# Hybrid attention block: the rotated key's halves from the latent turns, ten dummy products at the start, and rotary query stores from ScalarE

## The chip, the cores and the metric

The kernel runs on one core of a Trainium2 chip. A core has five engines, each with its own queue of instructions that it works off strictly in order: TensorE (PE in the profile, its weight loads PEld), VectorE (DVE), ScalarE (ACT), GpSimd (POOL) and SyncE (SP), which here does nothing but issue DMAs. The metric is the time of one execution in microseconds (us) on the device; lower is better.

## What is computed

One block with two attention branches over 512 tokens with 16 learned meta tokens ahead of them (528 positions, 16 heads, model width 1024). Cut to what matters here:

```python
u = rmsnorm(h, pre_norm_g[l])
proj = u @ w_in[l]
(cq, ckv, k_pe_raw, z_mla, fq, fk, fv, f_logit, z_fox, gate_a, gate_b) = jnp.split(proj, split_idx, axis=-1)
q = (rmsnorm(cq, mla_q_norm_g[l]) @ w_uq[l])        # per head: 64 plain and 32 rotary columns
kv = (rmsnorm(ckv, mla_kv_norm_g[l]) @ w_ukv[l])
k_pe = rope(k_pe_raw, pos)[:, None]                 # one rotated key of 32 columns for all heads
q_m = jnp.concatenate([q_nope, rope(q_pe, pos)], axis=-1)
k_m = jnp.concatenate([k_nope, jnp.broadcast_to(k_pe, ...)], axis=-1)
o_mla = causal_block_attention(q_m, k_m, v_mla, MLA_SCALE)
log_f = jax.nn.log_sigmoid(f_logit + fox_forget_b[l])
cum = jnp.cumsum(log_f, axis=-1)                    # added to the fox scores
o_fox = causal_block_attention(fox_heads(fq), fox_heads(fk), fox_heads(fv), FOX_SCALE, cum)
y_mla = (o_mla * jax.nn.silu(z_mla)) @ w_br_mla[l]
y_fox = (o_fox * jax.nn.silu(z_fox)) @ w_br_fox[l]
mixed = (jax.nn.sigmoid(gate_a) * y_mla + jax.nn.sigmoid(gate_b) * y_fox) @ w_out[l]
h = h + rmsnorm(mixed, post_norm_g[l])
```

## The kernel before

**Halves.** A float32 product is made of three products in a shorter format: an operand is split into an upper half (a rounded copy, names ending in h, hi or wh) and a lower half (the remainder, l, lo or wl). Each weight tile of 128 x 1024 is loaded raw by SyncE (`wload`, L90 for its DMA), copied into wh by ScalarE (L127) and subtracted into wl by GpSimd (L128, recorded at the helper's line L102). Raw and split weight tiles have three buffers each. `mm` (L96) and `tps` (L99) are all products and transposes, so tiles are told apart by name.

**Order.** TensorE's order is written out by hand: both large stages stand under a manual schedule, and a PE instruction runs where the program has it. On the other engines the framework's scheduler decides at build time, by priority (program order, which `tc.high_priority(offset=...)` raises) and by its own estimate of when an operand is ready. `tc.issue_after(ins)` puts an instruction behind `ins` on the same engine, `tc.keep_in_program_order` pins one. The list `behind` holds an instruction behind which the wh casts (L126) are put.

**First stage (L261 to L519).** Five token tiles (0 to 3 of 128 tokens, 4 of the 16 meta tokens) are loaded, normed (`squares`, `scaled`), turned on PE (`turn`, tile pt), scaled by the gain and split into uTh and uTl (`turned`). `small` makes the 432 narrow columns of the projection (tile psm: query latent, key-value latent, rotary key, forget logits). `back` norms the latents and rotates the key on the token-major tile sm. `latent` turns sm into the PSUM tile pc, which has one buffer, and copies out: cTh by ScalarE (L433), cTl by VectorE (L434), the rotated key kpT (L435) and the forget logits fT (L436) by ScalarE. Then come the fox queries and keys of head pair 0 (`qk`, tiles fq and fk): 7 of their steps, the last latent, the forget chain, and the rest. `hl_done` splits such a product into hlq or hlk: ScalarE copies the upper half (L239), VectorE subtracts the lower one (L240, recorded at L102), and only then is the accumulator free. There are three accumulators of 512 columns (`acc`), used in turn by all projections.

The forget chain is Abs, Exp, Ln on ScalarE (L503 to L505), a combination (L506) and a running sum (L507) on VectorE, two halves ch (L510, L511), four DMAs into the tile CT (L516) and two into DRAM (L518). CT enters the fox scores through a product with ONE, a tile that holds ones in two rows of each half.

**Start of attention (L534 to L566).** The rotated key must stand in two tiles of 128 partitions, one 64-row half for each head of a pair: KPH holds the upper half of kpT four times (four VectorE copies, L560), KPL the lower half twice over zeroed rows (GpSimd L561, VectorE L563). Then `pe_unit(0)` makes the rotary queries of the first eight heads (tile ppe): products, VectorE multiplications by the rotary tables (L623), GpSimd sums and halves (`rest`, L628 to L631) into gT. Head pair 0's part goes to the tile QP by DMA; the other six heads' part is stored to DRAM (`store`, L641; L90 qpe_dram) and loaded again for each later pair.

**Attention stages.** Sixteen stages alternate fox and MLA for eight head pairs. Each makes scores (st) into sf, exponentials (L763), normed probabilities as two half-precision parts pn (L777 to L791), and transposes these by DMA into pt (`dma_start_transpose`, eight a stage, in SyncE's queue); values (`ov`) multiply pt by vp one stage later. Between them PE works off weight products of later stages (z, fq, mq, v, ...) from a list `fills`, in pieces. In stage 1 (first MLA stage) the four stores of the rotary queries are issued by SyncE, behind the second store of ch.

The last stages multiply by the branch and output weights; the change does not touch them.

Of the kernel before, what the change touches and what calls it, by code (L numbers as in the profile page):

```python
# [54 lines left out]
def block_kernel(ctx: ExitStack, tc: tile.TileContext, x, meta_tokens, pre_norm_g, w_in, fox_forget_b,  # L55
# [21 lines left out]
    padp.tile([128, 56], F32, tag="pad", name="pad")  # L77
# [23 lines left out]
    def split_lo(eng, lo, src, hi):  # L101
        eng.tensor_tensor(out=lo, in0=src, in1=f32(hi), op=ALU.subtract)  # L102
# [120 lines left out]
    nc.gpsimd.memset(f32(CT), 0.0)  # L223
# [37 lines left out]
    with ExitStack() as ph:  # L261
# [57 lines left out]
        kpT = pal.tile([ROPE, L], F32, tag="kpT", name="kpT")  # L319
# [5 lines left out]
        hns, sts, pts0 = {}, {}, {}  # L325
# [73 lines left out]
        def back(t):  # L399
# [6 lines left out]
            for a, b, i in both:  # L406

                nc.scalar.activation(sm[:rows, a:b], psm[:rows, a:b], AF.Square, scale=(b - a) ** -0.5,
                                     accum_out=st2[:rows, i : i + 1])
# [14 lines left out]
        def latent(t, sm):  # L424
            rows, d0, q0 = (128, META + 128 * t, 0) if t < 4 else (META, 0, R_Q)
            k0 = R_Q + R_KV
            pc = pps.tile([128, 4, 128], F32, tag="pc", name=f"pc{t}", bufs=1)
            i0 = q0 // 128
            for i in range(i0, 3):
                tps(pc[:, i, :rows], sm[:rows, 128 * i : 128 * i + 128], ident[:rows, :rows])  # L430
            tps(pc[0 : ROPE + NH, 3, :rows], sm[:rows, k0:NSM], ident[:rows, :rows])
            ds = slice(d0, d0 + rows)
            nc.scalar.copy(cTh[:, i0:3, ds], pc[:, i0:3, :rows])  # L433
            split_lo(nc.vector, cTl[:, i0:3, ds], pc[:, i0:3, :rows], cTh[:, i0:3, ds])  # L434
            nc.scalar.copy(kpT[:, ds], pc[0:ROPE, 3, :rows])  # L435
            nc.scalar.activation(fT[:, ds], pc[ROPE : ROPE + NH, 3, :rows], AF.Identity, bias=fb)  # L436
# [27 lines left out]
        for c in (2, 3):  # L464
# [33 lines left out]
        qk = q_fox(0) + k_fox(0)  # L498
        run(qk[:7])
# [19 lines left out]
        run(qk[7:])  # L519
# [14 lines left out]
    with ExitStack() as att:  # L534
# [8 lines left out]
        KP = [ac.tile([128, L], F32R, tag=n, name=n) for n in ("KPH", "KPL")]  # L543
# [15 lines left out]
        for r in range(4):  # L559
            nc.vector.tensor_copy(KP[0][32 * r : 32 * r + 32], kpT)  # L560
        nc.gpsimd.memset(f32(KP[1]), 0.0)  # L561
        for h in range(2):
            split_lo(nc.vector, KP[1][64 * h : 64 * h + 32], kpT, KP[0][0:32])  # L563
        lctx.close()
        gpool = gctx.enter_context(tc.tile_pool(name="gpool", bufs=1, side="right"))
        gT = [gpool.tile([128, KD, S], F32, tag=n, name=n) for n in ("gT0", "gT1")]  # L566
# [25 lines left out]
        def pe_unit(g):  # L592
            if g == 0:
                r0, tt = (p.rearrange("p a b -> p (a b)")[:, 0 : 8 * S].bitcast(F32).rearrange("p (c s) -> p c s", c=4)
                          for p in pts)
            else:
                r0, tt = gT[0][:, 4:8], gT[1][:, 4:8]
            rp = r0[:, 0:2]

            rr = [r0[:, 2:4], tt[:, 2:4]] if g else [t[:, 4:6] for t in gT]  # L600
            if g == 0:
                nc.sync.dma_start(rp, rope_pe)
# [8 lines left out]
            def srcs():  # L611
                if g:

                    tc.keep_in_program_order(nc.sync.dma_start(rp, rope_pe))
# [3 lines left out]
            for xi in range(2):  # L618
                get = (lambda: half(1)) if xi else weights(srcs, lambda ws: half(0, ws))

                def done(i, ps, xi=xi):
                    for cs in range(2):
                        nc.vector.tensor_tensor(out=tt[:, 2 * xi + cs], in0=ps, in1=rp[:, cs], op=ALU.mult)  # L623
                out += unit(f"ppe{g}{xi}", get, cq_act, 2, REAL, done)

            def rest(x):

                nc.gpsimd.tensor_tensor(out=tt[:, x], in0=tt[:, x], in1=tt[:, 3 - x], op=(ALU.subtract, ALU.add)[x])  # L628
                hi, lo = rr[x][:, 0], rr[x][:, 1]
# [4 lines left out]
                else:  # L634

                    for h in range(2):
                        for i in range(2):
                            r = 64 * h + 32 * i + 16 * x
                            dma(f32(QP[r : r + 16]), rr[x][16 * h : 16 * h + 16, i])
# [197 lines left out]
        pe, rest0, store0 = pe_unit(0)  # L837
        pe_rest = [(0, lambda x=x: rest0(x)) for x in range(2)]
        g = gate_unit()
        first = pe + v + [(0, in_order)] + g[:4]  # L840
# [23 lines left out]
        run(first)  # L864
        late = []
        for si, (br, pr) in enumerate(stages):
# [6 lines left out]
            if si == 0:  # L873
# [187 lines left out]
```

## Time and profile before

| | us |
|---|---|
| three runs | 621.47, 623.43, 623.82 |
| their median | 623.43 |
| the profiled execution | 622.67 |
| its span, first to last instruction | 620.9 |
| TensorE busy in it | 598.2 |
| ScalarE, VectorE, GpSimd busy | 330.6, 315.9, 265.2 |

A row of the timeline gives the start in us from the span's beginning, the duration in us, engine, line, operation, written tile, read tiles, shapes and how many instructions are merged in it; the bracket at its end is the time that the engine sat idle before it and what ended that. Matmuls overlap: each row lasts longer than the distance to the next. SPq is SyncE's queue, in which a DMA's row is its issue, not its transfer. The page's clock row gives the share of full speed that TensorE was granted.

### The profile page before, as it was taken

To read this page: it belongs to the slowest core of one execution; us is meant where nothing else is said; L and a number is where in the kernel's file an instruction comes from. 1 tells how busy PE (TensorE), PEld (TensorE's weight loads), DVE (VectorE), ACT (ScalarE), POOL (GpSimd) and SP (SyncE) were. 2 spreads that over 40 slices of the span, in tenths; PEclk is the share of its full clock that TensorE was granted. 3 is DMA by queue.
4 is the path that set the end of the run, shared out by engine and by line. 5 is a ranking of instruction groups with operands and counts; after the bars stand their busy time and mean duration, and the time that the engine had idled before them with its cause. 6 is when DMAs were issued, how large, how long until landed. Compare 5 with 4: busy or idle time off the path is not lost.

```text
span 620.9 us, 11001 instructions
## 1 busy us (share of the span) xinstructions
PE 598.2 (96%) x3811; PEld 508.3 (82%) x3811; DVE 315.9 (51%) x922; ACT 330.6 (53%) x757; POOL 265.2 (43%) x270
## 2 busy tenths in 40 slices
PE   4997999799999999999999999999999999999996
PEld 4886889688889889889888898887888888888885
DVE  3948657456666765764675657627321122024034
ACT  7855746556665765775676658646322222232321
POOL 4216636344345653444353523542644444444610
PEclk9999999799999999999999999999999999999998
DMA  8431579968987778879778696971433332333602
GB/s 277 93 95 51 116 174 145 219 158 169 172 180 143 168 182 169 192 172 184 151 165 182 145 174 155 189 170 34 136 102 101 102 95 86 92 103 120 253 34 102
DMA packets 223512, 89.31 MB, mean 144 GB/s; under 512 B 141708, under 2 KB 216852, under 8 KB 223456
## 3 DMA queue, kind: packets, MB, share of 16 engines
q1 hardware_dynamic: 223456, 88.61, 61.9%
q8 instruction: 30, 0.49, 0.3%
q14 instruction: 26, 0.21, 0.1%
HBM read 54.43 MB, written 4.00 MB: 94 GB/s over the span
## 4 chain that ended last, share of the span: by engine, by line
PE 85%; DVE 5%; ACT 3%; DMA 2%; issue 2%; SPq 1%; POOL 1%; DVEq 0%; ACTq 0%; POOLq 0%
PE pg L96 14%; PE py L96 14%; PE z L96 14%; PE v L96 8%; PE po L96 7%; PE fq L96 6%; PE fk L96 6%; PE st L96 5%; PE ov L96 3%; PE psm L96 3%; DVE sf L755 2%; PE mq L96 2%; SPq L90 1%; PE mk L96 1%; DMA ht<-in_x_dram 1%
## 5 line engine op out<-in xcount | busy, mean ns | idle before, releaser
L102 POOL TENSOR_TENSOR wl<-wraw,wh 128x1024 fp32r<-128x1024 f32 (+1 forms) x90 | 207.2, 2306 | 222.6 <-ACT wh L127 220.8
L127 ACT CAST wh<-wraw 128x1024 fp32r<-128x1024 f32 (+1 forms) x90 | 90.0, 1004 | 170.0 <-issue 48.1
L763 ACT ACTIVATE sf<-sf,nb 128x144 f32<-128x144 f32 (+3 forms) x128 | 72.0, 565 | 13.8 <-DVE nb L755 13.8
L791 DVE SCALAR_TENSOR_TENSOR pn<-sf,ri,pn 128x128 f16<-128x128 f32 (+3 forms) x128 | 68.7, 575 | 13.1 <-ACT pn L790 13.0
L790 ACT ACTIVATE pn<-sf,ri 128x128 f16<-128x128 f32 (+3 forms) x128 | 61.5, 551 | 19.9 <-ACT sf L763 17.9
L944 DVE SCALAR_TENSOR_TENSOR tb<-th,py 128x512 f32<-128x512 f32 x16 | 11.0, 687 | 101.9 <-PE py L96 101.9
L96 PE MATMUL st<-hlk,hlq 64*128 64x272 f32 (+3 forms) x480 | 51.0, 311 | 0.7 <-DVE nb L755 0.2
L96 PE MATMUL z<-uTh,wh 128*128 128x512 f32 x128 | 50.8, 397 | 0.0
L755 DVE CUSTOM_DVE_ANT_0 sf<-st,maskt 128x272 f32<-128x272 f32 (+2 forms) x128 | 48.4, 434 | 3.9 <-PE st L96 3.9
L96 PE MATMUL pg<-uTh,wh 128*128 128x512 f32 x128 | 50.2, 392 | 0.0
L96 PE MATMUL z<-uTh,wl 128*128 128x512 f32 x128 | 50.0, 391 | 0.0
L96 PE MATMUL z<-uTl,wh 128*128 128x512 f32 x128 | 49.9, 390 | 0.0
L96 PE MATMUL pg<-uTl,wh 128*128 128x512 f32 x128 | 49.8, 389 | 0.0
L96 PE MATMUL pg<-uTh,wl 128*128 128x512 f32 x128 | 49.8, 389 | 0.0
L96 PE MATMUL py<-gh,wh 128*128 128x512 f32 x128 | 49.8, 389 | 0.0
L96 PE MATMUL py<-gl,wh 128*128 128x512 f32 x128 | 49.8, 389 | 0.0
L96 PE MATMUL py<-gh,wl 128*128 128x512 f32 x128 | 49.8, 389 | 0.0
L777 POOL TENSOR_TENSOR mt<-sf,ri 128x96 f32<-128x96 f32 (+1 forms) x32 | 9.5, 296 | 85.9 <-DVE ri L772 72.3
L96 PEld LDWEIGHTS st<-hlk,hlq 64*128 64x128 f32 x480 | 37.2, 187 | 8.1 <-ACT wh L127 2.5
L96 PE MATMUL v<-uTh,wh 128*128 128x256 f32 (+1 forms) x128 | 36.6, 286 | 2.3 <-DVE hlk L102 2.3
L96 PE MATMUL ov<-pt,vp 128*64 128x512 f16 (+4 forms) x416 | 35.2, 318 | 3.5 <-DMA pt<-pn 3.5
L96 PEld LDWEIGHTS <-vp 128*64 128x64 f16 (+1 forms) x416 | 22.8, 113 | 17.5 <-issue 8.5
(189 smaller groups left out, 1419.5 us busy)
## 6 DMA issues: line engine op xcount, KB each, us to landing
wraw<-in_w_in_dram SPq DMA_DIRECT2D x56, 512.0 KB
wraw<-in_w_br_fox_dram SPq DMA_DIRECT2D x8, 512.0 KB
wraw<-in_w_br_mla_dram SPq DMA_DIRECT2D x8, 512.0 KB
wraw<-in_w_out_dram SPq DMA_DIRECT2D x8, 512.0 KB
pt<-pn SPq DMA_TRANSPOSE x128
xr<-in_x_dram SPq DMA_DIRECT2D x4, 512.0 KB
out_dram<-yo SPq DMA_DIRECT2D x8, 256.0 KB
QP<-qpe_dram SPq DMA_DIRECT2D x7, 256.0 KB
```

The lines of the kernel that those rows point to most:

```text
L90: ins = (start or nc.sync.dma_start)(out=out, in_=src)
L96: nc.tensor.matmul(*a, **k)
L102: eng.tensor_tensor(out=lo, in0=src, in1=f32(hi), op=ALU.subtract)
L127: nc.scalar.copy(wh[:, :n], raw[:, :n])
L755: nc.vector.tensor_tensor_reduce(out=sf_of(h, b)[:, c0 : c0 + w], in0=ps[h][:, o : o + w], in1=maskt[:, m0 : m0 + w], scale=-scale, scalar ...
L763: exps[g] = nc.scalar.activation(sf, sf, AF.Exp, bias=sums["nb"][:, h, b : b + 1], scale=-1.0, accum_out=sums["su"][:, h, b : b + 1]).ins
L777: nc.gpsimd.tensor_tensor(out=mt, in0=src, in1=ri.unsqueeze(3).broadcast_to([128, 2, nb_, META]), op=ALU.mult)
L790: nc.scalar.activation(hi, sf, AF.Copy, scale=rib)
L791: nc.vector.scalar_tensor_tensor(out=lo, in0=sf, scalar=rib, in1=hi, op0=ALU.mult, op1=ALU.subtract)
L944: nc.vector.scalar_tensor_tensor(out=tb[br], in0=ths[i, br], scalar=1.0, in1=py, op0=ALU.add, op1=ALU.mult)
```

## The change

It has five parts.

1. CT and ONE are cleared by VectorE instead of GpSimd, and ten products of ONE with 512 columns of CT are put first on PE, into an accumulator that nobody reads. The gain column's copy moves behind the scaling of the first token tile.
2. KPH and KPL are allocated early. `latent` writes their first 32 partitions straight from pc: the upper half by ScalarE in place of the copy kpT, the lower half by VectorE. All five operations of `latent` get a priority raised by 60, with ScalarE's three ahead of VectorE's two. KPL is zeroed at the start.
3. The four copies and two subtractions of L559 to L563 go. Four DMAs from SyncE spread the first 32 partitions: three for KPH, one for KPL. They stand behind the rotary query products in the program, as does the allocation of gT, so `pe_unit` now looks its tiles up when it runs.
4. From the seventh fox step on, the wh casts are put behind the square of tile 1's latents, until the rotary query products are through. The rest of `qk` moves ahead of ch, and ch behind the copy of the second half of hlk. An Exp of one element follows it.
5. The four stores of the rotary queries are issued by ScalarE, at the end of stage 0, two behind the copy hlq and two behind the second copy hlk of the first MLA pair.

```diff
+    KP = [fx.tile([128, L], F32R, tag=n, name=n) for n in ("KPH", "KPL")]
-    nc.gpsimd.memset(f32(CT), 0.0)
-    nc.gpsimd.memset(f32(ONE), 0.0)
+    nc.vector.memset(f32(CT), 0.0)
+    nc.vector.memset(f32(ONE), 0.0)
     for h in range(2):
-        nc.gpsimd.memset(f32(ONE[64 * h : 64 * h + 2, :]), 1.0)
+        nc.vector.memset(f32(ONE[64 * h : 64 * h + 2, :]), 1.0)
+    nc.gpsimd.memset(f32(KP[1]), 0.0)
...
-            nc.scalar.copy(cTh[:, i0:3, ds], pc[:, i0:3, :rows])
-            split_lo(nc.vector, cTl[:, i0:3, ds], pc[:, i0:3, :rows], cTh[:, i0:3, ds])
-            nc.scalar.copy(kpT[:, ds], pc[0:ROPE, 3, :rows])
-            nc.scalar.activation(fT[:, ds], pc[ROPE : ROPE + NH, 3, :rows], AF.Identity, bias=fb)
+            with tc.high_priority(offset=60):
+                nc.scalar.copy(cTh[:, i0:3, ds], pc[:, i0:3, :rows])
+                nc.scalar.copy(KP[0][0:ROPE, ds], pc[0:ROPE, 3, :rows])
+                nc.scalar.activation(fT[:, ds], pc[ROPE : ROPE + NH, 3, :rows], AF.Identity, bias=fb)
+                split_lo(nc.vector, cTl[:, i0:3, ds], pc[:, i0:3, :rows], cTh[:, i0:3, ds])
+                split_lo(nc.vector, KP[1][0:ROPE, ds], pc[0:ROPE, 3, :rows], KP[0][0:ROPE, ds])
...
+        spun = acc("spun")
+        for _ in range(10):
+            mm(spun, ONE, CT[:, 0:512], start=True, stop=True)
         gps = ppt.tile([128, 4, 128], F32, tag="pt", name="gps")
         tps(gps[:, 0, 0:KD], g8, ident[0:KD, 0:KD])
         squares(0, pin)
+        scaled(0, pin)
         pin(nc.vector.tensor_copy(gcol, gps[:, 0, 0:KD]))
-        scaled(0, pin)
...
         qk = q_fox(0) + k_fox(0)
+        behind[:] = [squared[1]]
         run(qk[:7])
         latent(3, sms[3])
...
+        run(qk[7:])
         ch = pal.tile([NH, 2, L], F32R, tag="ch", name="ch")
-        nc.scalar.activation(ch[:, 0], fa[:, 0], AF.Copy, scale=-1.0 / SC_FOX)
+        with tc.issue_after(halved[("k", 1, 0), 1]):
+            nc.scalar.activation(ch[:, 0], fa[:, 0], AF.Copy, scale=-1.0 / SC_FOX)
+            nc.scalar.activation(pad[0:1, 0:1], eps_t[0:1, 0:1], AF.Exp)
...
-        run(qk[7:])
...
-        for r in range(4):
-            nc.vector.tensor_copy(KP[0][32 * r : 32 * r + 32], kpT)
-        nc.gpsimd.memset(f32(KP[1]), 0.0)
-        for h in range(2):
-            split_lo(nc.vector, KP[1][64 * h : 64 * h + 32], kpT, KP[0][0:32])
...
-            def store(x, a, b):
+            def store(x, a, b, start=None):
                 for i in range(2):
-                    dma(qpe_dram[8 * g + a : 8 * g + b, i, x], rr[x][16 * a : 16 * b, i])
+                    dma(qpe_dram[8 * g + a : 8 * g + b, i, x], results(x)[16 * a : 16 * b, i], start)
...
-        run(first)
+        run(pe0)
+        behind.clear()
+        for r in (64, 32, 96):
+            nc.sync.dma_start(f32(KP[0][r : r + ROPE]), f32(KP[0][0:ROPE]))
+        nc.sync.dma_start(f32(KP[1][64 : 64 + ROPE]), f32(KP[1][0:ROPE]))
...
+        run(first[len(pe0) :])
...
                 run(fill[5:])
+                written[0] = False
+                for x in range(2):
+                    with tc.issue_after((halved[("q", 0, 0), 0], halved[("k", 0, 0), 1])[x]):
+                        store0(x, 2, 8, nc.scalar.dma_start)
+                written[0] = True
             else:
                 run(fill[:1])
-                if si == 1:
-
-                    written[0] = True
-                    for x in range(2):
-                        store0(x, 2, 8)
-                    written[0] = False
```

More of the change, by code (lines that the diff above doesn't have):

```diff
@@ L101, in split_lo @@
     def split_lo(eng, lo, src, hi):
-        eng.tensor_tensor(out=lo, in0=src, in1=f32(hi), op=ALU.subtract)
+        return eng.tensor_tensor(out=lo, in0=src, in1=f32(hi), op=ALU.subtract)
     def wload(srcs):
@@ L542, in block_kernel @@
         QP = ac.tile([128, S], F32R, tag="QP", name="QP")
-        KP = [ac.tile([128, L], F32R, tag=n, name=n) for n in ("KPH", "KPL")]
         maskt = ac.tile([128, L + 16], BF16, tag="maskt", name="maskt")
@@ L558, in block_kernel @@
             nc.gpsimd.memset(pn[b // 3][:, :, PN_STEP * b % 15, :], 0.0)
[L559 to L566 removed]
+        gT = []
         wuqh = wuq.rearrange("p k (h e) -> p k h e", e=NOPE + ROPE)
@@ L592, in pe_unit, with room, results @@
         def pe_unit(g):
-            if g == 0:
[L594 to L602, printed above, removed]
+            def room():
+                if g == 0:
+                    return [p.rearrange("p a b -> p (a b)")[:, 0 : 8 * S].bitcast(F32).rearrange("p (c s) -> p c s", c=4)
+                            for p in pts]
+                return gT[0][:, 4:8], gT[1][:, 4:8]
+            def results(x):
+                if g == 0:
+                    return gT[x][:, 4:6]
+                return room()[x][:, 2:4]
+            if g == 0:
+                nc.sync.dma_start(room()[0][:, 0:2], rope_pe)
             out = []
@@ L863, in block_kernel @@
         ahead(first + sum(fills, []) + tail)
-        run(first)
+        run(pe0)
[3 more added lines that the diff above has]
+        nc.sync.dma_start(f32(KP[1][64 : 64 + ROPE]), f32(KP[1][0:ROPE]))
+        lctx.close()
+        gpool = gctx.enter_context(tc.tile_pool(name="gpool", bufs=1, side="right"))
+        gT += [gpool.tile([128, KD, S], F32, tag=n, name=n) for n in ("gT0", "gT1")]
+        run(first[len(pe0) :])
         late = []
```

23 lines of the change are left out of this document (12 added, 11 removed).

## The prediction

> **What bounds the kernel now.** I read the page's totals first, then the list of waits of TensorE, then the busy time by stretches, and only then single rows of the timeline.
>
> ```profile
> span 620.9 us, 11001 instructions
> PE 598.2 (96%) x3811; PEld 508.3 (82%) x3811; DVE 315.9 (51%) x922; ACT 330.6 (53%) x757; POOL 265.2 (43%) x270
> ...
> PE ov L96 <- DMA pt<-pn: 3.5, 2, 3.1
> ...
> PE v L96 <- DVE hlk L102: 2.3, 1, 2.3
> PE ppe L96 <- DVE hlk L102: 1.5, 1, 1.5
> PE pc L99 <- ACT fT L436: 1.1, 1, 1.1
> ...
> 48.00:68.00 20.00, 16.21 (x114) 14.21 (x114) 15.27 (x25) 10.03 (x15) 15.27 (x18) 1.00 0.35 96
> 113.00:123.00 10.00, 6.53 (x49) 4.57 (x45) 3.89 (x17) 6.59 (x19) 3.50 (x5) 0.66 1.11 253
> 123.00:580.00 457.00, 456.68 (x2931) 385.90 (x2932) 228.21 (x669) 242.49 (x525) 203.65 (x200) 1.00 0.65 148
> ```
>
> TensorE (PE) is the bound: 598.2 of 620.9 us. In the table by stretches (us, then PE, PEld, DVE, ACT, POOL, granted clock, DMA share, GB/s) it idles 0.3 us in the 457 us from 123 on. So a microsecond saved before 123 us reaches the end, unless something new stops PE later. The change touches only work before 123 us, where four places lose time: the start, a wait for the PSUM tile pc, two waits in 48 to 68, and the stretch 113 to 123, where the granted clock averages 0.66.
>
> **The change part by part.** *Dummies at the start.* Ten products of 512 columns now run first, on CT and ONE, whose clearing moves from GpSimd to VectorE.
>
> ```profile
> 0.93 0.54 POOL L223 MEMSET CT<- 128x528 f32 x1
> ...
> 10.20 1.97 PE L99 MATMUL pt<-ident,hn 128*128 128x128 f32 x8 [2.21 <-DVE hn L348]
> 11.82 0.71 PE L96 MATMUL psm<-wsh,uTh 128*128 128x432 f32 x1
> ...
> 27.00 1.04 PE L99 MATMUL pt<-ident,hn 128*128 128x128 f32 x8
> ```
>
> Eight transposes take 1.97 us at 10.20 and 1.04 us at 27.00, so PE starts slow, and a PE already fast at 10.20 would gain 0.9. The dummies can begin near 2 us (the clears: 0.54 and a few shorter ones) and at most last 10 x 0.71 = 7.1, to about 9. Most likely they end near 6, with about 4 us of little PE work left before 10.20; a stretch of 3.1 us without a product, below, was enough to halve the clock. I take -0.3; bounds -0.9 (they keep PE fast) and +1.2 (they end at 9 and push the first tile's transposes past 10.2). Swapping gcol and the scaling saves a copy of a tenth, hidden behind the second tile's load.
>
> *The latent turns.* All five copies out of pc get a high priority, ScalarE's three first, and the kpT copy becomes the copy into KPH.
>
> ```profile
> 28.48 0.45 ACT L433 CAST cTh<-pc 128x384 fp32r<-128x384 f32 x1
> ```
>
> pc has one buffer. Its first filling is copied only from 28.48, behind weight casts, and the second waited the 1.1 us listed above. With the copies ahead of the casts that wait should go: -1.0, bounds -1.1 and +0.3 (a lower half written on VectorE from PSUM, five more small operations in that chain). The casts that fall back are also held behind the second tile's square; their products start only at 39.8, about ten microseconds later, which covers it.
>
> *The rotated key.* Before, VectorE makes four copies and two subtractions of the whole key. They go; the spread to the other partitions becomes four DMAs.
>
> ```profile
> 47.99 4.03 DVE L560 CAST KPH<-kpT 32x528 fp32r<-32x528 f32 x4
> ...
> 51.64 0.40 PE L96 MATMUL ppe<-cTh,wh 128*128 128x512 f32 x1
> ...
> 52.79 1.41 DVE L102 TENSOR_TENSOR KPL<-kpT,KPH 32x528 fp32r<-32x528 f32 x2 [0.77 <-POOL KPL L561]
> ...
> 53.89 2.56 POOL L102 TENSOR_TENSOR wl<-wraw,wh 128x1024 fp32r<-128x1024 f32 x1 [1.13 <-ACT wh L127]
> 54.23 0.44 DVE L102 TENSOR_TENSOR hlk<-fk,hlk 128x272 fp32r<-128x272 f32 x1
> 54.59 2.42 DVE L506 SCALAR_TENSOR_TENSOR fa<-fT,fa 16x528 f32<-16x528 f32 x1
> ...
> 57.04 1.25 DVE L507 TENSOR_TENSOR_SCAN fa<-fa 16x528 f32<-16x528 f32 x1
> 58.22 0.39 DVE L102 TENSOR_TENSOR hlk<-fk,hlk 128x256 fp32r<-128x256 f32 x1
> ...
> 58.66 0.19 PEld L96 LDWEIGHTS v<-uTh,wh 128*128 128x128 f32 x1 [2.70 <-DVE hlk L102]
> 58.99 2.52 SPq L516 DMA_DIRECT2D CT<-ch  x4
> ...
> 59.13 0.69 DVE L511 SCALAR_TENSOR_TENSOR ch<-fa,ch 16x528 fp32r<-16x528 f32 x1
> ```
>
> There are three accumulators. The second rotary product needs the one that the first hlk subtraction frees (54.23), the value product the one that the second frees (58.22). Both subtractions stand behind the key's six operations, from 47.99 to 54.2, and the second behind the forget chain too. L506 took 2.42 us where its like, L511, took 0.69: it ended just after GpSimd's subtraction of 53.89, so the two seem to share a port, which the new lower half, reading PSUM, needs less. With six operations gone, the first subtraction comes right behind its copy and the second near 51 to 53, where PE reaches the values at about 53 in the new time. Both waits go: 1.5 + 2.3 = -3.8. Bounds: -4.1 (PE issues 12 products in 2.8 us from 51.64, so the slow restart goes as well) and -1.5 (L506 is still blocked and the second subtraction stays behind the scan). What would be late next is CT, whose first reader is the row of the chain of waits
>
> ```profile
> 67.51 1.19 PE st L96 x16
> ```
>
> (start, us): in the new time 67.5 - 0.3 - 1.0 - 3.8 = 62.4, and the DMAs that fill CT follow the scan, which moves up by as much. The four new DMAs cost SyncE about 0.6 each (2.52 for the four into CT), 2.5 in all, in a stretch where its queue stands nearly empty; the key is first read at 88.7. I take 0 for them, at worst CT 2.5 later, still covered. The early Exp table load moves work on ScalarE and saves nothing on PE.
>
> *The rotary query stores.* They leave SyncE's queue in stage 1 and are issued by ScalarE in stage 0, two behind the first MLA hlq copy and two behind the second hlk copy.
>
> ```profile
> 83.79 2.64 SPq L90 DMA_TRANSPOSE pt<-pn  x2
> ...
> 84.64 0.73 ACT L239 CAST hlk<-mk 128x272 fp32r<-128x272 f32 x2 [2.52 <-PE mk L96]
> 88.39 0.29 ACT L681 ACTIVATE vh<-v,vsc 128x32 f16<-128x32 f32 x1 [3.03 <-DVE vsc L676]
> ...
> 90.66 2.04 PE L96 MATMUL ov<-pt,vp 80*64 80x512 f16 x26
> 92.89 4.03 SPq L90 DMA_DIRECT2D qpe_dram<-gT  x4
> 94.05 0.50 PE L96 MATMUL fq<-uTh,wh 128*128 128x512 f32 x1
> 95.55 0.73 DVE L791 SCALAR_TENSOR_TENSOR pn<-sf,ri,pn 128x128 f16<-128x128 f32 x2
> ...
> 97.02 1.86 SPq L90 DMA_DIRECT2D wraw<-in_w_in_dram  x1
> 99.07 3.16 SPq L90 DMA_TRANSPOSE pt<-pn  x2
> ...
> 111.87 3.64 SPq L90 DMA_TRANSPOSE pt<-pn  x2
> 113.16 0.35 PE L96 MATMUL st<-CT,ONE 64*128 64x400 f32 x2
> 116.65 0.61 PE L96 MATMUL ov<-pt,vp 80*64 80x512 f16 x1 [3.14 <-DMA pt<-pn]
> 117.59 3.79 PE L96 MATMUL ov<-pt,vp 80*64 80x512 f16 x25 [0.33 <-DMA pt<-pn]
> 122.90 0.50 PE L96 MATMUL z<-uTh,wh 128*128 128x512 f32 x1
> ```
>
> In stage 1 the probabilities are ready to be transposed at 96.3 (95.55 + 0.73), but SyncE issues the four stores from 92.89 to 96.9, then a weight load, then the first transposes at 99.07, and the last end at 115.5. PE has nothing from 113.5 on, waits 3.14, and comes back at half clock: from 113.5 to 122.9 it does in 9.4 us what took 3.4 at the turn before (90.66 to 94.05). That costs 6.0. Without the stores the load fits in before 96.3 and the transposes start 2.8 us sooner; the first value product could start at 113.9 and the last transpose land near 114.8, in today's time. A wait of about 1 us is left, and waits of 1.5 and 2.3 us left the clock at 1.00 in 48 to 68. So -5.0; bounds 0 (something else holds the transposes) and -6.0.
>
> ScalarE issues four stores, each about the 1.0 us that SyncE's took (4.03 / 4). It does nothing between hlq and 84.64, and nothing from 85.4 to 88.39, so two stores fit in each gap: 0. Without that cover, each microsecond beyond 3 delays the values' halves.
>
> The Trainium skill, DMA: Bandwidth & Descriptors, "Issuing engines are not separate DMA queues", speaks against this move: a transfer issued by another engine runs on the same 16 DMA engines, and only the issuing sequencer's time is saved. This trace says that the sequencer's time is just what lacks, 4.03 us on SyncE; by the rule alone the bytes would still meet the transposes, now in stage 0, which is the second rival below.
>
> The sum: -0.3 - 1.0 - 3.8 - 5.0 = -10.1 against the profiled execution's 622.67 us (span 620.9 and 1.8 around it), so **612.6 us**. The median of the three runs, 623.43, is 0.8 above that execution, so the median may lie as much higher; I keep 612.6. Its own range: all gains at their far ends give 610.6, and the runs spread by 1 us, so 609.5 below; 615.5 above, where the start costs 0.3, the wait for pc stays, and the values still wait 1.3.
>
> **The rivals.** *The stall of stage 1 stays.* For it: after the stores SyncE works without a break from 99.07 to 115.5, so the shared DMA engines rather than its instructions may set the pace. Against it: the start of that row of work is plainly delayed by the stores. It gives 622.67 - 5.1 = 617.6.
>
> *The stall moves to stage 0.* The stores' 768 KB run beside the last transposes, issued until 86.4 and needed at 90.66. A transpose of stage 1 lands about 2 us after its issue (115.5 to 117.6), so 2.1 us of slack are left against 4.03 us of stores. If they land behind all of it, PE waits 2 to 3 us and falls to half clock, which costs about 6 as in stage 1: 618.6. Against it: the stores come in two halves, and only the last transposes meet them.
>
> *Slower: the sums come late.* ch now waits on ScalarE behind the second hlk copy, and a table load, casts that wait for weights and the Exp dummy can stand before or behind it; the DMAs into CT wait for ch, and the first scores wait for CT. With PE 5 us ahead, at 62.4, each microsecond that CT lands after that is lost, and beyond about 3 another 2.9 (6.0 - 3.1) by the clock. It decides from CT landing at 69.6, 6 us later than now (issued until 61.5, 2 us more): then the 10.1 are gone. At 72.5 the time is 625.6. For it: only that ScalarE's order is the framework's choice. Against it: every input of ch comes earlier.
>
> *The change does not do what it says.* The framework orders ScalarE, VectorE and SyncE by its own estimates; the subtractions could stay behind the forget chain and the stores behind other work, with all four terms near their weak bounds (0, 0, -1.5, 0): 621.2.
>
> **How the numbers follow.** Forecast 0.62, stall stays 0.14, stall moves 0.08, no effect 0.08, slower 0.08. 0.5% is 3.1 us, about what a measurement of this kernel can tell from no change: faster means under 619.6, which the first three cases are, 0.84; same 0.08; slower 0.08. The range 609.5 to 619.2 takes in the first three and leaves out 0.16.
>
> **What would show it.** Right: VectorE's row for L560 gone; no wait of PE for hlk between the rotary products and the values; no wait for pc; the stores on ScalarE's queue ahead of vh; the first pn transposes of stage 1 less than 1 us behind their subtraction; the granted clock at 1.00 from there to the end of the attention stages, and PE without idle time after them. Wrong: a wait of PE for pt or CT over 2 us anywhere between the first scores and the third stage, a dip of the clock beside it, or PE idle among the weight products because a cast has fallen back.

## The result, and the profile after

| | before | after |
|---|---|---|
| median, us (runs) | 623.41 (621.47 to 623.84, 6) | 617.21 (616.07 to 619.75, 6) |
| profiled execution, us | 622.67 | 616.33 |
| its span, us | 620.9 | 614.5 |

The ratio is 0.9911, with a 95% interval of 0.9886 to 0.9936: the kernel became about 0.9% faster. The forecast was 612.6 us, with a range of 609.5 to 619.2, so the direction and the range held, and the forecast's own value was 4.6 us too low. Where those microseconds are lost is the subject of what follows.

The page's totals after, then TensorE's waits (us in total, times, longest):

```profile
span 614.5 us, 11031 instructions
PE 600.5 (98%) x3821; PEld 508.9 (83%) x3821; DVE 311.5 (51%) x925; ACT 329.9 (54%) x758; POOL 264.1 (43%) x266
```

```profile
PE ov L96 <- DMA qpe_dram<-gT: 2.7, 1, 2.7
PE spun L96 <- DVE ONE L227: 2.1, 1, 2.1
...
PE v L96 <- DVE hlk L102: 0.4, 1, 0.4
PE pc L99 <- ACT uTh L373: 0.3, 1, 0.3
```

The wait for pc fell from 1.1 to 0.3, the wait ahead of ppe is gone and the one ahead of the values fell from 2.3 to 0.4. The wait for pt of 3.1 is gone too, but a wait of 2.7 stands in its place, ahead of the same kind of product (ov). The table by stretches (us, then PE, PEld, DVE, ACT, POOL, granted clock, DMA share, GB/s) says where:

```profile
82.00:86.00 4.00, 2.97 (x33) 2.14 (x31) 0.22 (x2) 0.00 (x0) 0.21 (x1) 1.00 1.11 159
86.00:88.00 2.00, 0.38 (x2) 0.21 (x4) 0.00 (x0) 0.00 (x0) 0.00 (x0) 0.87 1.13 336
88.00:90.00 2.00, 2.00 (x14) 1.25 (x12) 0.82 (x3) 1.63 (x5) 0.00 (x0) 0.50 0.61 171
90.00:92.00 2.00, 1.62 (x16) 1.20 (x12) 2.00 (x12) 1.70 (x5) 1.11 (x1) 0.78 0.18 65
92.00:113.00 21.00, 20.75 (x161) 19.07 (x163) 14.56 (x38) 14.08 (x33) 12.04 (x14) 1.00 0.78 157
113.00:123.00 10.00, 10.00 (x76) 7.85 (x73) 7.82 (x32) 8.29 (x24) 4.39 (x9) 1.00 1.13 226
```

The stretch from 113 on, which had a clock of 0.66 before, is full at 1.00. The half clock now sits in 86 to 92, in the turn from stage 0 (first fox stage) to stage 1. Rows of the timeline there, for TensorE, SyncE's queue, and ScalarE with its queue (ACTq):

```profile
82.27 0.56 PE L96 MATMUL st<-hlk,hlq 64*128 64x144 f32 x6
...
84.56 0.40 PE L96 MATMUL ov<-pt,vp 80*64 80x512 f16 x1
87.62 3.61 PE L96 MATMUL ov<-pt,vp 80*64 80x512 f16 x25 [2.66 <-DMA qpe_dram<-gT]
...
93.79 0.50 PE L96 MATMUL fq<-uTh,wh 128*128 128x512 f32 x1
```

```profile
68.39 13.32 SPq L90 DMA_TRANSPOSE pt<-pn  x8
81.77 2.32 SPq L90 DMA_DIRECT2D wraw<-in_w_in_dram  x2
```

```profile
75.66 2.10 ACTq L90 DMA_DIRECT2D qpe_dram<-gT  x2
...
80.67 7.65 ACTq L90 DMA_DIRECT2D qpe_dram<-gT  x2
88.37 0.29 ACT L687 ACTIVATE vh<-v,vsc 128x32 f16<-128x32 f32 x1 [9.11 <-DMA pt<-pn]
```

The wait of 2.66 is put down to a store, but ov reads only pt and vp; the transposes into pt are what it needs, and the chain below has the last of them land at 87.53, just ahead of 87.62.

From the first MLA scores to the first fq of stage 1, TensorE took 5.68 us before (88.37 to 94.05) and takes 11.52 now (82.27 to 93.79). So 5.84 us are lost there, and in absolute time fq stands 0.26 earlier than before: all that the first 80 us had won is gone. The second pair of stores holds ScalarE's queue for 7.65 us. The chain of waits (start, us) shows behind what:

```profile
78.41 9.12 DMA pt<-pn
...
87.56 0.02 ACTq L90
...
87.61 0.71 ACTq L90
...
88.37 0.29 ACT L687 ACTIVATE vh<-v,vsc 128x32 f16<-128x32 f32 x1 [9.11 <-DMA pt<-pn]
```

The last transpose of stage 0, issued by SyncE at 78.41, lands 9.1 us later, and ScalarE's fourth store goes out only then. The issues of the third and fourth store take 0.71 us each; the rest of the 7.65 is this wait. The instruction list explains why one queue waits for the other: the framework gives every DMA of SyncE and ScalarE one of eight completion counters (DMAHW0 to 7) in turn, and a DMA first waits for that counter's last user. From the list of the changed kernel, the last transpose (counter 5) and ScalarE's second pair:

```
59 L90 DMA_TRANSPOSE pt_723<-pn_721 128x9x128 [waits DMAHW5_49,DVE_49]
111 L90 DMA qpe_dram<-gT_775 6x16x512 [waits DMAHW3_49]
112 L90 DMA qpe_dram<-gT_775 6x16x512 [waits DMAHW5_49,Pool_49]
```

There were thus two candidates for the 5.84 us: the bytes, which delay the transposes that TensorE waits for, and ScalarE's wait, which delays the halves of the values and the exponentials of stage 1.

### The profile page after: what moved, and what is told of

Same layout as the page of the kernel before. It is cut to its first block, busy times and chain, and to the rows that moved or that the text cites. A ratio compares the mean times of both kernels' runs of the same rounds, so it can differ in the third digit from the quotient of the medians.

```text
span 614.5 us, 11031 instructions
## 1 busy us (share of the span) xinstructions
PE 600.5 (98%) x3821; PEld 508.9 (83%) x3821; DVE 311.5 (51%) x925; ACT 329.9 (54%) x758; POOL 264.1 (43%) x266
## 4 chain that ended last, share of the span: by engine, by line
PE 85%; ACT 4%; DVE 4%; issue 3%; DMA 2%; POOL 1%; SPq 0%; ACTq 0%; DVEq 0%; POOLq 0%
PE py L96 14%; PE z L96 14%; PE pg L96 14%; PE po L96 7%; PE fk L96 7%; PE v L96 7%; PE fq L96 6%; PE st L96 6%; PE ov L96 4%; DVE sf L761 2%; PE psm L96 2%; PE mq L96 2%; DMA pt<-pn 1%; ACT uTh L373 1%; PE mk L96 1%
## 5 line engine op out<-in xcount | busy, mean ns | idle before, releaser
L96 PE MATMUL ov<-pt,vp 128*64 128x256 f16 (+4 forms) x416 | 35.1, 317 | 2.7 <-DMA qpe_dram<-gT 2.7
```

The costliest lines, as they stand in the source:

```text
L96: nc.tensor.matmul(*a, **k)
```

## The experiments

Two distances on TensorE sum each run up. Turn 1 runs from the first MLA scores to the first fq of stage 1, turn 2 from the first scores of stage 2 to the z products behind them (111.55 to 116.57 in the changed kernel). Without a stall they take 5.68 and 5.02 us. From that z to the end the profiles take 498 to 500 us, except E4 (503) and E8 (506).

| run | median, us | ratio to before (95%) | turn 1 | turn 2 |
|---|---|---|---|---|
| before | 623.41 | 1 | 5.68 | 11.34 |
| changed kernel | 617.21 | 0.9911 (0.9886, 0.9936) | 11.52 | 5.02 |
| E1 no early stores | 612.43 | 0.9846 (0.9816, 0.9875) | 5.68 | 5.84 |
| E2 stores back | 615.22 | 0.9883 (0.9855, 0.9911) | 5.68 | 9.87 |
| E3 stores behind the transposes | 612.97 | 0.985 (0.9823, 0.9878) | 5.68 | 8.81 |
| E4 before, with the stores moved | 621.62 | 0.9983 (0.9958, 1.0008) | 9.09 | 5.02 |
| E6 small stores | 613.1 | 0.9856 (0.9833, 0.9879) | 5.68 | 5.91 |
| E7 stores all early | 617.21 | 0.9927 (0.9901, 0.9952) | 7.09 | 5.02 |
| E8 stores in two parts | 618.71 | 0.9939 (0.9919, 0.996) | 5.68 | 6.55 |
| E12 E3, key by VectorE | 613.1 | 0.9864 (0.9837, 0.9892) | 5.68 | 9.16 |
| E10 E3, no dummies | 615.81 | 0.9893 (0.9869, 0.9916) | 5.68 | 9.66 |
| E11 E3, no priority | 615.53 | 0.9901 (0.9882, 0.9919) | 5.68 | 6.87 |
| E15 E3, old key | 616.35 | 0.991 (0.9889, 0.9931) | 5.68 | 6.58 |
| E14 stores by GpSimd | 614.32 | 0.9883 (0.9859, 0.9907) | 5.68 | 6.86 |

The kernel before was run again beside each group of experiments and took 623.41 beside the changed kernel, 622.68 beside E1 to E4, 622.56 beside E6, E7, E8 and E12, and 621.5 beside the last four: between groups the ratios are to be compared.

**E1, the stores left out.**

```diff
-                for x in range(2):
-                    with tc.issue_after((halved[("q", 0, 0), 0], halved[("k", 0, 0), 1])[x]):
-                        store0(x, 2, 8, nc.scalar.dma_start)
...
-                if pr:
+                if pr > 3:
                     load_qp(pr)
```

> The changed kernel without the four early stores of the rotary queries; pairs 1 to 3 go on with pair 0's rotary queries, so their loads are left out too (the scores of six MLA heads are not the reference's). Theory A (the stores' new place makes the stall between stage 0 and stage 1, by sharing the DMA engines with the last transposes and by holding ScalarE): first fq of stage 1 about 5.7 us after the first MLA scores as before, not 11.5; no half clock in 86 to 92; 617.2 - 5.8 = 611.4 us. Theory B (TensorE only ran 6 us ahead of SyncE's transposes of stage 0, which would stop it with or without the stores): first fq stays 10 us or more behind the first MLA scores, 616 to 618 us.

Theory A came true: turn 1 is back at 5.68, and the ratio falls by 0.0065, about 4 us. TensorE was not simply ahead of SyncE's transposes. Some 1.8 of the 5.8 expected are missing: a remnant of 0.8 us stays in turn 2 even without a store, and the profiled execution reached the first MLA scores 1 us later (83.24 against 82.27).

**E2, the stores back on SyncE in stage 1.** 
```diff
-                        store0(x, 2, 8, nc.scalar.dma_start)
...
                 run(fill[:1])
+                if si == 1:
+                    written[0] = True
+                    for x in range(2):
+                        store0(x, 2, 8)
+                    written[0] = False
                 run(fill[1:5])
```

> The changed kernel with the stores back where they were, on SyncE in stage 1. Theory A: the stall of stage 0 is gone (a gain of 5.8) and the one of stage 1 is back (a loss of 6.0): 617.4 us, with the half clock at about 107 to 117 in place of 88 to 91. Theory B: the stall of stage 0 stays and the one of stage 1 comes back on top, or the row of stage 1 has the slack of the lost time: 621 to 623.5 us.

The places are those of theory A: turn 1 without a stall, turn 2 with one again. The time, 615.22, is 2.2 below what was expected, since the returning stall costs 4.85 (9.87 - 5.02), not 6.3, and the kernel before, run beside E2, took 0.7 less than the value from which the expectation was worked out.

**E3, the stores from SyncE behind stage 0's last transpose.**

```diff
-                    with tc.issue_after((halved[("q", 0, 0), 0], halved[("k", 0, 0), 1])[x]):
-                        store0(x, 2, 8, nc.scalar.dma_start)
+                    with tc.issue_after(through[0]):
+                        store0(x, 2, 8)
```

> The changed kernel with the four stores issued by SyncE, behind the last transpose of stage 0 (ahead of the loads of the forget sums and of the values' transpose). Theory A: no store meets the transposes of stage 0 and ScalarE is held by none; SyncE's queue has some 4 us of stores before stage 1's probabilities are ready: about 611 to 612.5 us, first fq about 5.7 us behind the first MLA scores. Theory B: 616 to 618 us, TensorE waits for pt in the turn to stage 1 as in the changed kernel.

E3 beats both kernels: its interval lies wholly below the changed kernel's. SyncE's queue and TensorE in it:

```profile
80.19 1.20 SPq L90 DMA_DIRECT2D wraw<-in_w_in_dram  x2
81.44 5.15 SPq L90 DMA_DIRECT2D qpe_dram<-gT  x4
...
91.68 3.19 SPq L90 DMA_TRANSPOSE pt<-pn  x2
...
109.32 0.38 PE L96 MATMUL ov<-pt,vp 80*64 80x512 f16 x1 [1.40 <-DMA pt<-pn]
110.09 2.77 PE L96 MATMUL ov<-pt,vp 80*64 80x512 f16 x25 [0.40 <-DMA pt<-pn]
```

The stores fill a hole in which SyncE has little to do, between the transposes of two stages. They still push the first transposes of stage 1 about 1 us back, and this profile keeps a stall of 3.8 us in turn 2. It was E3's slowest execution (614.63; the others took 612.3 to 613.2), so most of its executions probably lose less there.

**E4, the kernel before with the fifth part alone.**

```diff
                 first_t.extend(through)
                 run(fill[5:])
+                written[0] = False
+                for x in range(2):
+                    with tc.issue_after((halved[("q", 0, 0), 0], halved[("k", 0, 0), 1])[x]):
+                        store0(x, 2, 8, nc.scalar.dma_start)
+                written[0] = True
...
-                if si == 1:
-                    written[0] = True
-                    for x in range(2):
-                        store0(x, 2, 8)
-                    written[0] = False
```

> The kernel before with this one edit alone: the four stores issued by ScalarE in stage 0. Theory A: stage 1 wins its 6.0 us, but the turn to stage 1 loses 4 to 6, since the stores again run beside the last transposes of stage 0 and ScalarE's last store waits for one of them: 621.5 to 623.5 us. Theory B: TensorE is not 6 us ahead here, so there is no new stall in stage 0 and the whole gain of stage 1 shows: 617.4 us.

Turn 1 loses 3.41 and turn 2 wins 6.32, as theory A has it. The loss comes through ScalarE here:

```profile
90.74 2.01 PE L96 MATMUL ov<-pt,vp 80*64 80x512 f16 x25 [0.19 <-DMA pt<-pn]
...
91.53 0.29 ACT L681 ACTIVATE vh<-v,vsc 128x32 f16<-128x32 f32 x1 [6.68 <-DMA pt<-pn]
...
94.59 0.39 PE L96 MATMUL st<-hlk,hlq 64*128 64x272 f32 x1 [1.84 <-DVE nb L755]
```

The transposes are late by only 0.19 for TensorE, but ScalarE's queue is held until the last of them has landed. Its first half of the values starts at 91.53 (88.39 in the kernel before), VectorE's work on the scores stands behind that, and TensorE waits 1.84 for a score buffer.

The median is not the clean sum of these: the twelve executions lie in two groups, 619.5 to 621.0 and 622.3 to 624.9. The profiled one (624.1) has a further stall in a late stage that no other profile here shows:

```profile
267.42 0.38 PE L96 MATMUL ov<-pt,vp 80*64 80x512 f16 x1 [1.33 <-issue]
269.17 3.45 PE L96 MATMUL ov<-pt,vp 80*64 80x512 f16 x25 [1.38 <-DMA pt<-pn]
```

Its cause stays open. Up to the first z of stage 2 this kernel was 3.2 ahead of the one before, which fits the lower group.

**E6, the same stores with a sixth of the bytes.**

```diff
-                        store0(x, 2, 8, nc.scalar.dma_start)
+                        store0(x, 2, 3, nc.scalar.dma_start)
```

> The changed kernel with its four ScalarE stores in the same places, but each moves one head instead of six (1/6 of the bytes); pairs 1 to 3 keep pair 0's rotary queries and their loads are left out (the scores of six MLA heads are not the reference's). Theory D (the bytes of the stores make the last transposes of stage 0 land late, and ScalarE's wait only passes that on): the second pair is issued in about 2 us, no wait of TensorE for pt over 0.5 us, first fq 5.7 to 6.2 us behind the first MLA scores, 611.5 to 613 us. Theory C (ScalarE's fourth store waits for another queue's transpose whatever the bytes, and that makes the stall): the second pair still takes over 5 us and the values' halves come as late, 616 to 617.5 us.

```profile
68.68 11.16 SPq L90 DMA_TRANSPOSE pt<-pn  x8
...
79.15 3.14 ACTq L90 DMA_DIRECT2D qpe_dram<-gT  x2
...
84.76 2.04 PE L96 MATMUL ov<-pt,vp 80*64 80x512 f16 x26
```

Theory D: with few bytes the eight transposes are issued in 11.2 us instead of 13.3 and land in time, and the same wait on the counter costs ScalarE 3.14 us, which harms nobody. The bytes are the root, and ScalarE's wait passes the lateness on, as in E4.

**E7, all four stores behind hlq.**

```diff
-                    with tc.issue_after((halved[("q", 0, 0), 0], halved[("k", 0, 0), 1])[x]):
+                    with tc.issue_after(halved[("q", 0, 0), 0]):
```

> The changed kernel with all four stores behind the first MLA hlq copy (about 75.7), so that none of them is queued behind a late transpose, but all 768 KB meet the transposes of stage 0. Theory D (bytes): the transposes are issued until 82 and land late, TensorE waits 1.5 to 3 us for pt and falls to half clock, the turn stays at 9 to 11.5 us: 615 to 617.5 us. Theory C (ScalarE's wait): the values' halves are back at about 83, the turn takes 5.7 to 6.5 us: 611.5 to 613 us.

```profile
68.80 14.76 SPq L90 DMA_TRANSPOSE pt<-pn  x8
...
76.00 6.32 ACTq L90 DMA_DIRECT2D qpe_dram<-gT  x4
...
83.27 0.39 PE L96 MATMUL v<-cTh,wh 128*128 128x272 f32 x1 [2.69 <-DVE hlk L102]
```

The edit does not do what was expected of it: the fourth store still stands behind a transpose. It shares its counter with the sixth one, issued at 75.77, and the chain of waits has it go out when that one lands:

```profile
75.77 5.76 DMA pt<-pn
...
81.55 0.02 ACTq L90
```

So the 6.32 us are four issues of 0.7 to 1.3 us each and some 2.3 of waiting for the counter. The time is that of theory D, but hardly by its path: the transposes are stretched to 14.76 us, yet TensorE waits only 1.04 for pt, at full clock, and turn 1 takes 7.09, between what the two theories expect. The larger loss lies ahead of it: the hlk copies stand behind the stores, and TensorE waits 2.69 for an accumulator before it reaches the scores. E7 thus does not tell the two theories apart; E6 does. What E7 shows is that a ScalarE queue with work for TensorE in it is a bad place for stores.

**E8, the stores in two parts.**

```diff
-                        store0(x, 2, 8)
+                        store0(x, 2, 4)
...
                 n1()
+                if si == 1:
+                    for x in range(2):
+                        with tc.issue_after(through[0]):
+                            store0(x, 4, 8)
```

> Stores by SyncE in two parts: heads 2 and 3 behind the last transpose of stage 0, heads 4 to 7 behind the last transpose of stage 1. The version with all of them behind stage 0 took 612.97 us and kept a stall of 3.8 us in the turn from stage 1 to stage 2 (TensorE waits 1.4 and 0.4 us, then half clock). If the stores' bytes ahead of stage 1's transposes make that stall, it shrinks to 0.8 (as without any stores) and the time is 610 to 611.5 us; if SyncE's instruction time does it (eight stores instead of four, the first four still ahead of those transposes), it stays: 612.5 to 613.5 us. If the late part meets the transposes of stage 2, there is a new wait for pt in the turn to stage 3.

```profile
107.51 3.05 SPq L90 DMA_DIRECT2D qpe_dram<-gT  x4
...
132.22 0.38 PE L96 MATMUL ov<-pt,vp 80*64 80x512 f16 x1 [3.20 <-DMA pt<-pn]
```

The places are as expected, the time is not: turn 2 shrinks to 6.55 (5.84 was expected), and the late part pushes back the transposes of stage 2, so that TensorE stalls one turn later, for 3.2 us and at half clock. The hole behind stage 1's transposes has no room; the one behind stage 0's has most of what the four stores need.

**E12 and E15, the key taken back to VectorE.** E12 replaces the four spreading DMAs by VectorE copies; E15 restores the whole key of before (kpT, four copies, two subtractions). Both build on E3.

```diff
-        for r in (64, 32, 96):
-            nc.sync.dma_start(f32(KP[0][r : r + ROPE]), f32(KP[0][0:ROPE]))
-        nc.sync.dma_start(f32(KP[1][64 : 64 + ROPE]), f32(KP[1][0:ROPE]))
...
+        for r in (64, 32, 96):
+            nc.vector.tensor_copy(KP[0][r : r + ROPE], f32(KP[0][0:ROPE]))
+        nc.vector.tensor_copy(KP[1][64 : 64 + ROPE], f32(KP[1][0:ROPE]))
```

> The version with SyncE's stores behind the last transpose of stage 0 (612.97 us), with the spread of the rotated key taken back from the DMA to VectorE: three copies of the upper half and one of the lower, ahead of the first hlk subtraction. Theory of the prediction (those operations hold the two hlk subtractions, and TensorE waits for their accumulators): four copies of 1.0 us each; waits of TensorE for hlk ahead of ppe and v of 1.5 to 3.5 us together, 615 to 616.5 us. Rival (VectorE has the slack now that the forget chain is not blocked): under 1 us of waits, 613 to 614 us.

And E15, against E3 as well:

```diff
-                nc.scalar.copy(KP[0][0:ROPE, ds], pc[0:ROPE, 3, :rows])
+                nc.scalar.copy(kpT[:, ds], pc[0:ROPE, 3, :rows])
...
-                split_lo(nc.vector, KP[1][0:ROPE, ds], pc[0:ROPE, 3, :rows], KP[0][0:ROPE, ds])
...
+        for r in range(4):
+            nc.vector.tensor_copy(KP[0][32 * r : 32 * r + 32], kpT)
+        for h in range(2):
+            split_lo(nc.vector, KP[1][64 * h : 64 * h + 32], kpT, KP[0][0:32])
```

> The same version with the whole rotated key of before: the turns copy it to kpT on ScalarE, and VectorE makes the four copies and two subtractions at the old place, no DMA. Theory of the prediction (VectorE's key work by itself holds the hlk subtractions): waits of TensorE for hlk of 3 us and more ahead of the second rotary product and the values come back, 616 to 617 us. Rival, after the run with four of these operations, which made no wait: what cost the 3.8 us was that the key work began late (kpT's last copy behind a weight cast and hlq) and that the forget chain was blocked for 2.4 us; here kpT is copied early, six operations end near 51 to 52, at most 1 us of waits, 613 to 614 us.

In E12 the rival holds: no wait more than in E3, and 613.1 us. In E15 the prediction's theory holds: a wait of 0.4 ahead of ppe and 2.6 ahead of the values, turn 1 begins 3.7 later than in E3, 616.35 us. VectorE and GpSimd tell the two apart, E12 first:

```profile
51.51 1.25 DVE L514 TENSOR_TENSOR_SCAN fa<-fa 16x528 f32<-16x528 f32 x1
...
51.70 3.25 POOL L102 TENSOR_TENSOR wl<-wraw,wh 128x1024 fp32r<-128x1024 f32 x1 [2.68 <-ACT wh L127]
```

```profile
50.78 2.80 POOL L102 TENSOR_TENSOR wl<-wraw,wh 128x1024 fp32r<-128x1024 f32 x1 [2.67 <-ACT wh L127]
...
51.44 3.24 DVE L514 TENSOR_TENSOR_SCAN fa<-fa 16x528 f32<-16x528 f32 x1
...
55.05 0.39 PE L96 MATMUL v<-uTh,wh 128*128 128x272 f32 x1 [2.59 <-DVE hlk L102]
```

In E12 the scan starts 0.19 us ahead of GpSimd's subtraction, takes 1.25, and GpSimd takes 3.25. In E15 it starts 0.66 behind and takes 3.24. Two of the three microseconds are this collision, which the six operations on VectorE bring about here and the four miss by 0.19 us. So the DMA spread shows no gain of its own (612.97 against 613.1). What wins is that the lower halves are written turn by turn, which takes two operations out of this place; how much of that hangs on the 0.19 us, one pair of runs does not show.

**E10 and E11, E3 without the dummies and without the priority.** E10:

```diff
-        spun = acc("spun")
-        for _ in range(10):
-            mm(spun, ONE, CT[:, 0:512], start=True, stop=True)
```

> The version with SyncE's stores behind the last transpose of stage 0 (612.97 us), without the ten dummy products. If they keep TensorE fast through the first two tiles' transposes, the second tile's eight take 1.97 us again instead of 1.09 and the first psm product 0.71 instead of 0.44: first psm 1.1 later, 614.1 us. If the start hangs on the second tile's load and scaling alone, 612.5 to 613.3 us.

E11:

```diff
-            with tc.high_priority(offset=60):
+            with nullcontext():
                 nc.scalar.copy(cTh[:, i0:3, ds], pc[:, i0:3, :rows])
```

> The same version without the high priority of the latent turns' copies. Theory of the prediction: the copies out of pc fall behind other work of ScalarE again and the second filling waits about 1 us: second pc and all behind it 0.8 later, 613.8 us. Rival: the new order in which the copies are written (ScalarE's three first) does it by itself: second pc where it was, 612.5 to 613.3 us.

Without the dummies the first tiles' transposes are slow again, and the rotary products start 1.2 later than in E3 (50.69 against 49.47); the median is 2.8 higher (0.0043 in the ratio), part of it by a larger stall in turn 2. Without the priority the second pc waits longer than it ever did before:

```profile
PE pc L99 <- DVE KPL L102: 2.2, 1, 2.2
```

It starts 1.85 later (31.14 against 29.29), and what it waits for is the key's lower half on VectorE, the work that the change adds there. The prediction's theory has the place, then, but neither the engine nor the size: the ratio is 0.0051 above E3's, some 3 us, and 1.85 of them are seen at this place.

**E14, the stores issued by GpSimd,** behind its last small operation of the MLA values (`vscale`).

```diff
-                    with tc.issue_after((halved[("q", 0, 0), 0], halved[("k", 0, 0), 1])[x]):
-                        store0(x, 2, 8, nc.scalar.dma_start)
+                    with tc.issue_after(vscale[0]):
+                        store0(x, 2, 8, nc.gpsimd.dma_start)
```

> The changed kernel with the four stores issued by GpSimd, behind its last small operation of the MLA values of stage 0 (about 82.6, after SyncE's last transpose there), so that neither ScalarE nor SyncE issues them. If what is left of the stall in the turn to stage 2 (8.8 us against 5.0, with SyncE's stores) is SyncE's instruction time, the first transposes of stage 1 start within 0.6 us of their probabilities, the turn takes 5 to 6 us, 610.5 to 611.5 us. If it is the bytes, or if GpSimd takes long to issue them and the lower halves of the weights at 85.3 come late, 613 us or more, with a wait of TensorE for pt or wl.

```profile
82.42 2.60 POOL L91 DMA_DIRECT2D qpe_dram<-gT  x4
```

GpSimd issues the four in 2.6 us, and the lower halves of the weights are not late. Yet SyncE's first transposes of stage 1 start at 90.96, 8.6 us behind the first MLA scores (8.9 in E3), since SyncE's transpose of vh takes 4.34 us beside the stores; turn 2 takes 6.86. The profiled execution is the shortest of all the profiled ones (span 610.5), but the median is no better than E3's by the ratio. Neither theory is settled by this run.

## Why the prediction was right, and where it was not

Term by term, in the distances of TensorE's rows:

- **Start, taken as -0.3; measured about -1.9** at the third tile's transposes (18.50 against 20.36). The dummies keep TensorE fast, which was the lower bound's case (-0.9); E10 gives them alone some 1.2. The rest is that the first loads landed earlier: the second tile's transposes start at 8.73 against 10.20, and at 8.84 in E10, without dummies. Whether the change has a part in that is not shown. The term was mis-sized, and its lower bound was too high.
- **Wait for pc, -1.0; measured -0.8.** E11 adds that the priority pays for more than the old wait.
- **Rotated key, -3.8; measured -3.6** (ppe to v: 7.02 before, 3.39 after). The two rows of waits named it, and the place is right. E15 brings the waits back with the six operations (0.4 and 2.6), though two of these three microseconds are the scan's collision and not the six themselves. That the spread by DMA is needed, E12 does not bear out.
- **Stage 1, -5.0; measured -6.3** (turn 2 from 11.34 to 5.02): a little beyond the far bound of -6.0.
- **The stores on ScalarE, 0; measured +5.84.** This step failed: "so two stores fit in each gap: 0", and with it the argument against the second rival, "the stores come in two halves, and only the last transposes meet them". That rival had the mechanism, the wait of 2 to 3 us (2.66), the half clock and the price of about 6, and it was given 0.08; it lacked only the second path, ScalarE's wait. Two things were overlooked. Only the last transposes decide when TensorE may go on, so it is no comfort that just these meet the stores. And a store costs ScalarE more than its issue of about 1.0 us: the first pair took 2.10, the second 7.65, since the fourth store waits for the counter of the last transpose, which the stores slow. The prediction's own sign of being wrong, a wait for pt over 2 us with a dip of the clock beside it, did occur.

The sum -1.9 - 0.8 - 3.6 + 5.8 - 6.3 = -6.8 is within 0.5 of the measured -6.34 (622.67 to 616.33); the rest was lost between these places, 0.19 ahead of the first MLA scores and 0.25 ahead of the first scores of stage 2. The range held because it reached out to that rival, and with some luck: the start and stage 1 came out 2.9 better than forecast, and without that the profiled execution would stand at about 619.2, the end of the range. Had the forecast been weighed by the rule that the prediction cited, it would have come closer: the Trainium skill, DMA: Bandwidth & Descriptors, "Issuing engines are not separate DMA queues", has it that another issuer saves only the sequencer's time. SyncE's 4 us were saved and the bytes met the transposes, as E6 shows by taking the bytes away.

The slower rival did not occur: the first fox scores start at 61.22, 6.3 earlier than before, without a wait for CT. Nor did the one by which the change does nothing.

## What to carry to other kernels

Before a transfer is moved out of one stage's critical stretch, ask which transfers it will meet in its new place and how much slack their last one has; a stall that moves by one stage keeps its price, here with the clock's share of it. Of the places tried with all the bytes, the one that costs least is behind the last urgent transfer and ahead of the next, in the queue that issues both (E3), and a queue whose engine still has work for the bottleneck is the wrong one (E7). A transfer can also wait for another queue's: it is worth looking up which completion counter each one shares (E4, E7). An operation added to a chain, like the key's lower half behind pc, needs its priority checked together with it.

## What the runs showed of the hardware

- A wait's length alone did not set the clock. E3's waits of 1.40 and 0.40 around one product halved it, while E7's single 2.69 left it at 1.00. In each of the fourteen traces all changes of the granted clock lie whole multiples of 3.41 us apart, so a wait can be read by how it falls into such steps. Laid from the first rise of each trace, the steps after which the clock was halved have TensorE busy for 1.61 us or less, and those after which it stayed full for 1.57 or more (that one in E4; the next is 1.65). From half clock it rose after 2.85 or more and not after 2.65 or less. E3's two waits lie in one step, and E7's is divided by the end of a step at 81.82 (columns as above, E3 first, then E7):

```profile
107.81:111.22 3.41, 1.61 (x15) 0.87 (x15) 1.77 (x10) 3.25 (x10) 2.12 (x1) 1.00 1.12 275
111.22:114.64 3.42, 3.42 (x33) 3.11 (x28) 1.89 (x7) 2.91 (x10) 1.40 (x5) 0.50 1.30 267
```

```profile
78.40:81.82 3.42, 2.18 (x13) 1.57 (x11) 0.00 (x0) 0.00 (x0) 0.00 (x0) 1.00 0.95 134
81.82:85.23 3.41, 1.96 (x11) 1.78 (x12) 1.94 (x7) 0.66 (x2) 0.00 (x0) 1.00 1.60 111
```

  This is read off the traces, whose TensorE rows have modelled ends; no run was made to test it. The prediction's "waits of 1.5 and 2.3 us left the clock at 1.00" was no safe measure: the 2.26 there is divided by the end of a step at 57.42, and E15's 2.59, all in one step, halved the clock.
- VectorE's scan and GpSimd's subtraction hardly share time: the scan took 1.25 us where it started first and 3.24 where it started second, and the subtraction 3.25 and 2.80 (2.4 where nothing met it). The Trainium skill, SBUF — State Buffer, "Who interferes with whom", has it that a VectorE instruction with two SBUF inputs contends with a GpSimd instruction that reads SBUF, and that the order of issue decides which one is blocked. The two runs agree with it.
- Eight 128 x 128 transposes on TensorE took 1.09 us behind the dummies and 1.97 without them (E10): the dummies' fast clock lasted through the transposes.
- The issue of one store took 0.71 to 1.30 us on ScalarE (the changed kernel and E7), 0.71 to 2.27 on SyncE (E3) and 0.60 to 0.81 on GpSimd (E14). What ScalarE's rows of 7.65 and 6.32 us hold beyond that is the wait for a counter.
